# Memory scores at a place of their own, V's transposes in another PSUM bank, shifted start eighths for the first halves, and query loads of later chunks on SyncE's queue

## The chip, the cores and the metric

The kernel runs on one core of a Trainium2 chip. The metric is the device time of one execution in microseconds. In the text PE is TensorE's matmul stream, PEld its weight loads, DVE VectorE, ACT ScalarE, POOL GpSimd and SP SyncE.

## What is computed

One layer of a decoder, float32. Cut to what matters here (one sequence of 4096 tokens, d_model 1024; 64 sample tokens, the keys and values of the memory and the state of the convolution are treated beside it):

```python
h = rmsnorm(x, g_pre);  z = h @ w_in          # one projection, columns split in groups
out_a = silu(cg) * cb * conv3(cc * ch)        # 256 channels
out_b = silu(ag) * window_attention(q, k, v)  # 8 query heads, 2 kv heads, head_dim 64,
                                              # window 128, blocks of 128 queries, sink per head
out_c = silu(mg) * memory_attention(mq, mk, mv)  # 4 heads, 256 memory tokens
y = concat(out_a, out_b, out_c) @ w_out
return x + rmsnorm(y, g_post)
```

Window attention takes for each block of 128 queries the keys of this block and of the one before, masks them to a band, and adds a sink logit per head to the softmax. Memory attention is a plain softmax over 256 keys.

## The kernel before

**Stages.** The first 930 us or so are the input projection (lines 368 and 375): x is normalised and multiplied with `w_in` in three passes over groups of columns, in a seven-product scheme for blocks of 2 x 2, with every operand split into a high and a low float32r part. It writes to DRAM: `qd` (queries, keys, memory queries, as high and low parts), `vd` (V, transposed), `md` (the gates, and the finished convolution group). The attention of chunk 0 runs inside it. The last stage, from about 930 us to the end, is the output projection of all tokens with the attention of chunks 1 to 15 woven in.

**Chunks, halves, blocks, eighths.** A chunk c is 256 tokens. Half h = 2c + i is the attention of 128 of them (i is 0 or 1). A block is 128 rows of the output projection: `Block.run` multiplies a block with `w_out` in two parts of 512 columns (p = 0, 1), each with eight k steps of three matmuls of 512 columns (line 1602, tile y). A block has therefore 16 steps (p, k), called eighths here since each is an eighth of a part, and 48 matmuls. Before such a step the functions that are due are called: `starts_of(i)` looks them up by the running number 16 i + 8 p + k.

**What a half does.** `first_half(h)` and `second_half(h)` hold it. The first half of the work:

- `memory_transposes` of half h - 1 (tile xt, line 1352): the memory probabilities xp are transposed on TensorE into a PSUM bank pair of tag x, and copied out by VectorE and ScalarE (xpt, line 1356).
- `window_scores` of half h (ws, line 1318): 16 matmuls into two bank pairs of tag w.
- `products` of half h - 1 (wo, lines 1376, 1382 and 1057): probabilities times values, window and memory, into a bank pair of tag x.
- In a chunk's first half, two TensorE transposes that turn V's tile vT into tokens by channels (line 1654); they go into the unused end of the bank pair of the products, and ScalarE copies them out with a factor 0.5 (vt, line 1664).
- `window_probabilities` of half h: ScalarE copies the scores (sm, line 1327), VectorE merges the band (1328) and takes maxima (1266, 1268), ScalarE the exponentials (1274), VectorE the shares (1279 to 1282). In their midst the block before is finished (`finish_block(True)`, line 1624: row scaling and residual, in xr). `gates` (lines 1240, 1393) multiplies the products into the tile mix.
- the loads of the next chunk (`chunk_load`), or of the mix tile of the next chunk.

The second part:

- `memory_scores` (xs, line 1340): eight matmuls into a bank pair of tag x; maxima on VectorE (xmx, line 1155; negated in xnm, line 1156), exponentials on ScalarE (xp, line 1164), the reciprocal on VectorE (xrd, line 1170), the scaling on POOL (line 1176).
- `window_turns` (wt, line 1364): eight transposes of the window probabilities into a bank pair of tag w, ScalarE copies them (wpt, line 1292), and POOL masks them into two triangles (wpv and wpt, lines 1297 and 1300). The products of the next first half read both.

There are two bank pairs of tag w, one of tag x, and two single banks of tag z for y. So in the x pair xt, wo and xs follow one another in turn.

**Order.** TensorE runs in the order written (a manual schedule up to block 25); the other engines' orders, and SP's and POOL's queues, come from a list scheduler at build time. Each queue works in its order, and a DMA that waits holds up what is behind it. The split of the next block's mix tile into high and low parts (mh on ScalarE, line 1583; ml on VectorE, line 1584) is also started from `starts_of`.

**Loads.** Even chunks keep their keys (kst) and queries (q) in one buffer each, odd chunks in another, so that the loads of chunk c + 1 wait for the last reads of chunk c - 1. Keys and queries go by POOL's DMA queue (four DMAs, line 1086, and six of 256 KB, line 1099), vT, mix, xr and the output stores by SP's (lines 1089, 1108, 1569, 1627).

Of the kernel before, what the change touches and what calls it, by code (L numbers as in the profile page):

```python
# [15 lines left out]
P = 128  # L16
# [10 lines left out]
CT = 256  # L27
NCH = 4096 // CT
# [19 lines left out]
def f(ap):  # L48
    return ap.bitcast(F32)
# [3 lines left out]
def hybrid_layer(ctx: ExitStack, tc: tile.TileContext, a: dict):  # L53
    nc = tc.nc
    TE, V, S, G, DMA = nc.tensor, nc.vector, nc.scalar, nc.gpsimd, nc.sync
# [7 lines left out]
    ident = const.tile([P, P], F32, name="ident")  # L63
# [939 lines left out]
    chunks = {}  # L1003
# [37 lines left out]
    def two_banks(tag, name):  # L1041
        return ps[tag].tile([P, 2, 512], F32, tag=tag, name=name)
# [23 lines left out]
    class Chunk:  # L1066
# [24 lines left out]
        def load_queries(self):  # L1091

            self.q = self.pool("q").tile([P, 12, CT], F32R, tag="q", name=f"q{self.c}")
            heads = lambda part, j, ts: qd[part, j : j + 2, :, ts].rearrange("j (v d) n -> d j v n", v=2)
            for part in range(2):

                for n, (i, j) in enumerate(((0, 1), (4, 3), (8, 5))):
                    half = (n == 2) ^ part
                    G.dma_start(self.q[64 * half : 64 * half + 64, i : i + 4, :].rearrange("p (j v) n -> p j v n", v=2),  # L1099
                                heads(part, j, self.ts))  # L1100

        def load_mix(self):

# [291 lines left out]
    def chunk_load(c):  # L1395
        if c < NCH:
            chunks[c] = Chunk(c)

            chunks[c].load_queries() if c == 2 else chunks[c].load_keys()
            chunks[c].load_keys() if c == 2 else chunks[c].load_queries()  # L1400
# [238 lines left out]
    def first_half(h):  # L1639

        c, i = divmod(h, 2)
        before = (chunks[(h - 1) // 2], (h - 1) % 2) if 2 < h <= 2 * NCH else None
        if before:
            before[0].memory_transposes(before[1])
        if c < NCH:
            chunks[c].window_scores(i)
        banks = before[0].products(before[1]) if before else None
        new_v = c < NCH and i == 0
        if new_v:
            chunks[c].values(chunks[c - 1].vts[2])  # L1650
            banks = two_banks("x", f"vtp{c}") if banks is None else banks
            t = [banks[:, 1, CT + n * P : CT + n * P + P] for n in range(2)]
            for n in range(2):
                TE.transpose(t[n], chunks[c].vT[:, n * P : n * P + P], ident)
        soon = first_at[h] > 16 * (h - 3) + 4
        if before and soon:
            before[0].gates(before[1], banks)
        if c < NCH:
            chunks[c].window_probabilities(i)
        if before and not soon:  # L1660
            before[0].gates(before[1], banks)
        if new_v:
            for n in range(2):
                S.mul(chunks[c].vts[1 + n], t[n], 0.5)
            chunk_load(c + 1)
        elif c + 1 < NCH:
            chunks[c + 1].load_mix()

    def second_half(h):

        c, i = divmod(h, 2)
        if c < NCH:
            chunks[c].memory_scores(i)
            chunks[c].window_turns(i)


    first_at = {2: 4, 3: 21, 4: 35, 5: 47, 6: 59, 7: 71} | {h: 16 * (h - 3) + 4 for h in range(8, 2 * NCH + 1)}
    second_at = {2: 14, 3: 27, 4: 40, 5: 52, 6: 64, 7: 76} | {h: first_at[h] + 8 for h in range(8, 2 * NCH + 1)}

    def starts_of(i):  # L1680

        at = [(n, lambda h=h: first_half(h)) for h, n in first_at.items()] + [(n, lambda h=h: second_half(h)) for h, n in second_at.items()]
        if i + 1 < len(blocks) and blocks[i + 1].b != 32:
            at.append((max(16 * i, first_at.get(i + 2, 0) + 2), blocks[i + 1].split))
        return {(p, k): lambda now=now: [fn() for fn in now] for p in range(2) for k in range(8)
                if (now := [fn for n, fn in at if n == 16 * i + 8 * p + k])}
# [26 lines left out]
    for i in range(31):  # L1713
        if i == 26:
            turn.close()
        starts = starts_of(i)
        for step in ((p, k) for p in range(2) for k in (1, 3)) if i >= 26 else ():
            starts[step] = lambda before=starts.get(step, lambda: None): (before(), late())
        run(i, starts)
    for stage in stages:  # L1720
        for _ in stage:
            pass
    run(31, starts_of(31))
    run(32, {})
    finish_block()
# [106 lines left out]
```

## Time and profile before

| | us |
|---|---|
| Runs shown | 1541.38, 1549.06, 1551.43 (median 1549.06) |
| The profiled execution, whole | 1542.05 |
| Its span, first to last instruction | 1540.3 |
| TensorE matmuls busy | 1520.7 |
| TensorE weight loads busy (beside the matmuls) | 1397.0 |
| VectorE, ScalarE, POOL busy | 1137.5, 791.0, 393.2 |

How it is read: the profile comes from one execution, and its sums are sums of that execution. TensorE's busy time includes the modelled end of each matmul, which overlaps the next one, so the mean of a matmul is longer than the distance between two. The profile's waits are attributed to the instruction that released last. A weight load (PEld) precedes its matmul and runs beside the matmul before it, so that a wait for an operand of a transpose shows first in the weight loads. In a window's row stand, after the two ends, the length, then busy time (and instructions) of PE, PEld, DVE, ACT and POOL, the granted TensorE clock, the busy share of the DMA engines, and GB/s.

### The profile page before, as it was taken

Reading aid. Unit: us, or ns where it says so; the run is one execution under the profiler, and the core shown is the slowest. Engines: PE = TensorE matmul, PEld = TensorE weight load, DVE = VectorE, ACT = ScalarE, POOL = GpSimd, SP = SyncE. Lnnn points to the kernel's source line nnn. Section 1 sums busy time; section 2 is a strip of 40 time slices with the busy share of each in tenths; the row PEclk is TensorE's granted clock in tenths of the full one; section 3 lists DMA queues with packets and bytes.
Section 4 is the critical chain, followed back from the end, with each engine's and each line's share of the span. In section 5 each row is a group of like instructions: output and inputs, shape, how many; then the busy total and the mean of one; then the engine's idle time right before and its main releaser. Section 6 shows DMA issues by size and latency. Waiting matters only on the chain.

```text
span 1540.3 us, 30416 instructions
## 1 busy us (share of the span) xinstructions
PE 1520.7 (99%) x11581; PEld 1397.0 (91%) x11581; DVE 1137.5 (74%) x1965; ACT 791.0 (51%) x1949; POOL 393.2 (26%) x635
## 2 busy tenths in 40 slices
PE   9999999999999999999999999999999999999998
PEld 9999999999999999999999998778888888888776
DVE  6789887899988777897677678666666666666653
ACT  6686665476222222445454456555555555555541
POOL 0223232211400000000101203554444444445410
PEclk9999999999999999999999999999999999999999
DMA  9999999878755333678876889967777666666332
GB/s 258 177 240 232 278 284 263 276 241 292 193 180 180 126 126 126 236 223 281 244 269 204 238 295 272 208 140 155 156 155 161 149 149 160 148 148 150 124 123 96
DMA packets 178453, 306.29 MB, mean 199 GB/s; under 512 B 34437, under 2 KB 108165, under 8 KB 178277
## 3 DMA queue, kind: packets, MB, share of 16 engines
q1 hardware_dynamic: 130901, 227.38, 48.2%
q0 software_dynamic: 46688, 75.93, 23.5%
q8 instruction: 91, 1.49, 0.4%
q10 hardware_dynamic: 720, 1.05, 0.2%
q14 instruction: 53, 0.43, 0.1%
HBM read 197.23 MB, written 108.05 MB: 198 GB/s over the span
## 4 chain that ended last, share of the span: by engine, by line
PE 76%; DMA 7%; DVE 5%; POOL 5%; ACT 4%; issue 3%; ACTq 0%; SPq 0%; DVEq 0%; POOLq 0%
PE c L368 47%; PE y L1602 15%; DMA nat<-in_x_p 3%; PE ws L1318 3%; POOL xp L1176 3%; PE wo L1382 2%; PE wo L1057 2%; PE xs L1340 1%; PE wt L1364 1%; PE xt L1352 1%; DMA md<-th 1%; PE wo L1376 1%; POOL wpt L1300 1%; ACT xp L1164 1%; DMA x_0B<-in_xt 1%
## 5 line engine op out<-in xcount | busy, mean ns | idle before, releaser
L1602 PE MATMUL y<-wo,mh 128*128 128x512 f32 (+1 forms) x1040 | 336.1, 394 | 0.0
L375 DVE TENSOR_TENSOR z<-c,z 128x520 f32<-128x520 f32 (+1 forms) x308 | 194.8, 646 | 82.2 <-PE c L368 80.3
L1602 PEld LDWEIGHTS y<-wo,mh 128*128 128x128 f32 x1040 | 194.3, 188 | 42.3 <-issue 4.4
L1602 PE MATMUL y<-wo,ml 128*128 128x512 f32 (+1 forms) x520 | 201.4, 387 | 0.0
L1274 ACT ACTIVATE sm<-sm,wnm 128x128 f32<-128x128 f32 x256 | 99.4, 390 | 70.4 <-DVE wnm L1268 70.4
L1602 PEld LDWEIGHTS y<-wo,ml 128*128 128x128 f32 x520 | 98.0, 188 | 17.7
L1099 POOL DMA_DIRECT2D q<-qd x96 | 59.8, 631 | 139.2 <-PE wt L1364 81.6
L1176 POOL TENSOR_SCALAR xp<-xp,xrd 128x256 f32<-128x256 f32 x128 | 84.9, 675 | 34.8 <-DVE xrd L1170 34.7
L1297 POOL TENSOR_SCALAR_AFFINE_SELECT wpv<-wpt 128x512 f32<-128x512 f32 x62 | 40.4, 665 | 145.4 <-ACT wpt L1292 145.3
L1328 DVE COPY_PREDICATED sm<-wmask,ws 128x512 f32<-128x512 uint8 x60 | 40.6, 732 | 38.2 <-ACT sm L1327 38.2
L737 POOL CAST wmask<-negs 128x256 uint8<-128x256 f32 x1 | 0.9, 930 | 265.8 <-DMA negs<-in_wmask 265.8
L1292 ACT COPY wpt<-wt 128x512 f32<-128x512 f32 x64 | 34.6, 589 | 64.2 <-PE wt L1364 64.2
L1164 ACT ACTIVATE xp<-xs,xnm 128x256 f32<-128x256 f32 x128 | 59.4, 488 | 9.0 <-DVE xnm L1156 6.7
L1155 DVE TENSOR_REDUCE xmx<-xs 128x2 f32<-128x512 f32 x64 | 41.5, 686 | 29.9 <-PE xs L1340 29.8
L1356 ACT COPY xpt<-xt 128x512 f32<-128x512 f32 x30 | 17.6, 586 | 87.3 <-DVE xpt L1356 87.3
L1609 DVE TENSOR_TENSOR yn<-y,gpost 128x512 f32<-128x512 f32 (+1 forms) x66 | 45.1, 683 | 22.1 <-PE y L1602 22.0
L1318 PE MATMUL ws<-kst,q 128*128 128x256 f32 (+1 forms) x480 | 55.8, 298 | 0.0
L276 ACT ACTIVATE nat<-nat 104x1024 f32<-104x1024 f32 x40 | 42.3, 1058 | 26.1 <-DMA nat<-in_x_p 26.1
L1610 ACT ACTIVATE y<-y 128x512 f32<-128x512 f32 (+1 forms) x66 | 39.3, 595 | 30.2 <-DVE yn L1609 30.2
L1300 POOL TENSOR_SCALAR_AFFINE_SELECT wpt<-wpt 128x512 f32<-128x512 f32 x64 | 42.1, 669 | 43.3 <-ACT wpt L1292 43.1
L1356 DVE COPY xpt<-xt 128x512 f32<-128x512 f32 x30 | 20.8, 692 | 42.5 <-PE xt L1352 42.4
L1086 POOL DMA_DIRECT2D kst<-qd x64 | 38.8, 625 | 51.5 <-issue 24.8
(976 smaller groups left out, 5135.5 us busy)
## 6 DMA issues: line engine op xcount, KB each, us to landing
q<-qd POOLq DMA_DIRECT2D x96, 256.0 KB, 4.7
xr<-in_x_p SPq DMA_DIRECT2D x32, 512.0 KB
nat<-in_x_p SPq DMA_DIRECT2D x39, 416.0 KB
o_yp<-xr SPq DMA_DIRECT2D x31, 512.0 KB
md<-th POOLq DMA_DIRECT2D x48, 260.0 KB, 6.6
qd<-zh SPq DMA_DIRECT2D x48, 260.0 KB
qd<-z SPq DMA_DIRECT2D x48, 260.0 KB
kst<-qd POOLq DMA_DIRECT2D x60, 192.0 KB, 4.6
```

What stands on the lines that cost most here:

```text
L276: S.activation(t[:RG], t[:RG], AF.Square, accum_out=r[:RG, i : i + 1])
L368: TE.matmul(bank[:, :HW], l, r, start=first and i == 0, stop=last and i == 3 * KH - 1)
L375: add = lambda dst, other: V.tensor_tensor(dst, c, other, op=ALU.add)
L1099: G.dma_start(self.q[64 * half : 64 * half + 64, i : i + 4, :].rearrange("p (j v) n -> p j v n", v=2), heads(part, j, self.ts))
L1155: V.tensor_reduce(mx[:, :nb], s, axis=AX.X, op=ALU.max)
L1164: S.activation(p[:, i, :], s[:, i, :], AF.Exp, bias=nm[:, i : i + 1], scale=SCALE, accum_out=den[:, i : i + 1])
L1176: G.tensor_scalar(p[:, i, :], p[:, i, :], self.rds[h][:, i : i + 1], 0.5, op0=ALU.mult, op1=ALU.mult)
L1274: S.activation(sm[:, hh, :], sm[:, hh, :], AF.Exp, bias=nm[:, hh : hh + 1], scale=SCALE, accum_out=den[:, hh : hh + 1])
L1300: G.affine_select(p3, p3, pattern=[[0, 4], [1, P]], compare_op=ALU.is_ge, fill=0.0, base=0, channel_multiplier=-1)
L1318: TE.matmul(out(kvh, col, bank), q(kvh, col, bank)[r], k(kvh, part)[r], start=first, stop=True, skip_group_check=not first, **place)
L1602: TE.matmul(acc, self.hl[l][:, k], wo[k][c0 // 512][:, r, c0 % 512 : c0 % 512 + c1 - c0], start=j == 0, stop=j == passes * KT - 1)
L1609: V.tensor_tensor(yn[:m, c0:c1], acc[:m], gpost[:m, c0:c1], op=ALU.mult)
```

## The change

Four edits, all in the last stage:

1. `memory_scores` leaves `second_half` and becomes `memory_half(h)`, which is called at a time of its own: six eighths after the first half from h = 8 on (the second half stays at eight), five (seven for h = 2) before that.
2. V's transposes leave `first_half` and stand in `second_half` behind `window_turns`, in a bank pair of tag w instead of the end of a pair of tag x. Their copies on ScalarE stand right behind them.
3. The start eighths of halves 3 to 5, and the second starts of halves 4 to 7, are shifted. From half 8 on first and second starts are the same.
4. The six query loads of chunks 2 to 15 are issued on SP's queue; those of chunks 0 and 1 stay with POOL.

```diff
@@ load_queries
                     half = (n == 2) ^ part
-                    G.dma_start(self.q[64 * half : 64 * half + 64, i : i + 4, :].rearrange("p (j v) n -> p j v n", v=2),
-                                heads(part, j, self.ts))
+                    dst, src = self.q[64 * half : 64 * half + 64, i : i + 4, :].rearrange("p (j v) n -> p j v n", v=2), heads(part, j, self.ts)
+                    if self.c > 1:
+                        DMA.dma_start(f(dst), f(src))
+                    else:
+                        G.dma_start(dst, src)
@@ first_half
         banks = before[0].products(before[1]) if before else None
-        new_v = c < NCH and i == 0
-        if new_v:
-            chunks[c].values(chunks[c - 1].vts[2])
-            banks = two_banks("x", f"vtp{c}") if banks is None else banks
-            t = [banks[:, 1, CT + n * P : CT + n * P + P] for n in range(2)]
-            for n in range(2):
-                TE.transpose(t[n], chunks[c].vT[:, n * P : n * P + P], ident)
...
-        if new_v:
-            for n in range(2):
-                S.mul(chunks[c].vts[1 + n], t[n], 0.5)
+        if c < NCH and i == 0:
             chunk_load(c + 1)
...
-    def second_half(h):
+    def memory_half(h):
 
         c, i = divmod(h, 2)
         if c < NCH:
             chunks[c].memory_scores(i)
+
+    def second_half(h):
+
+        c, i = divmod(h, 2)
+        if c < NCH:
+            if i == 0:
+                chunks[c].values(chunks[c - 1].vts[2])
             chunks[c].window_turns(i)
+            if i == 0:
+                t = two_banks("w", f"vtp{c}")[:, 0].rearrange("p (a n) -> p a n", a=4)
+                for n in range(2):
+                    TE.transpose(t[:, n], chunks[c].vT[:, n * P : n * P + P], ident)
+                for n in range(2):
+                    S.mul(chunks[c].vts[1 + n], t[:, n], 0.5)
...
-    first_at = {2: 4, 3: 21, 4: 35, 5: 47, 6: 59, 7: 71} | {h: 16 * (h - 3) + 4 for h in range(8, 2 * NCH + 1)}
-    second_at = {2: 14, 3: 27, 4: 40, 5: 52, 6: 64, 7: 76} | {h: first_at[h] + 8 for h in range(8, 2 * NCH + 1)}
+    first_at = {2: 4, 3: 19, 4: 33, 5: 46, 6: 59, 7: 71} | {h: 16 * (h - 3) + 4 for h in range(8, 2 * NCH + 1)}
+    memory_at = {2: 11, 3: 24, 4: 38, 5: 51, 6: 64, 7: 76} | {h: first_at[h] + 6 for h in range(8, 2 * NCH + 1)}
+    second_at = {2: 14, 3: 27, 4: 41, 5: 54, 6: 67, 7: 79} | {h: first_at[h] + 8 for h in range(8, 2 * NCH + 1)}
...
+        at += [(n, lambda h=h: memory_half(h)) for h, n in memory_at.items()]
```

On TensorE the order of a half from 8 on was: xt, ws, wo, (V's transposes), 24 y matmuls, xs, wt, 24 y. It becomes: xt, ws, wo, 18 y, xs, 6 y, wt, (V's transposes), 24 y. In ScalarE's built order the copies of wt now stand behind the exponentials of the memory scores, and in POOL's order the scaling of xp stands ahead of the four masks.

More of the change, by code (lines that the diff above doesn't have):

```diff
@@ L1667, in first_half @@
             chunks[c + 1].load_mix()
+    def memory_half(h):
+        c, i = divmod(h, 2)
+        if c < NCH:
+            chunks[c].memory_scores(i)
     def second_half(h):
@@ L1672, in second_half @@
         if c < NCH:
-            chunks[c].memory_scores(i)
+            if i == 0:
+                chunks[c].values(chunks[c - 1].vts[2])
             chunks[c].window_turns(i)
-    first_at = {2: 4, 3: 21, 4: 35, 5: 47, 6: 59, 7: 71} | {h: 16 * (h - 3) + 4 for h in range(8, 2 * NCH + 1)}
-    second_at = {2: 14, 3: 27, 4: 40, 5: 52, 6: 64, 7: 76} | {h: first_at[h] + 8 for h in range(8, 2 * NCH + 1)}
+            if i == 0:
[7 more added lines that the diff above has]
+    second_at = {2: 14, 3: 27, 4: 41, 5: 54, 6: 67, 7: 79} | {h: first_at[h] + 8 for h in range(8, 2 * NCH + 1)}
     def starts_of(i):
         at = [(n, lambda h=h: first_half(h)) for h, n in first_at.items()] + [(n, lambda h=h: second_half(h)) for h, n in second_at.items()]
+        at += [(n, lambda h=h: memory_half(h)) for h, n in memory_at.items()]
         if i + 1 < len(blocks) and blocks[i + 1].b != 32:
```

## The prediction

> **What bounds the kernel now.** I read the page first, then busy time by stage, then who held up TensorE's weight loads, then the timelines of the last stage. A "half" below is the attention work of 128 tokens. Its TensorE sections carry the tile names xt (transposes of the memory probabilities), ws (window scores), wo (products), xs (memory scores) and wt (transposes of the window probabilities); y, the output projection, runs between them.
>
> ```profile
> span 1540.3 us, 30416 instructions
> PE 1520.7 (99%) x11581; PEld 1397.0 (91%) x11581; DVE 1137.5 (74%) x1965; ACT 791.0 (51%) x1949; POOL 393.2 (26%) x635
> ...
> 929.00:1035.00 106.00, 101.28 (x666) 81.58 (x665) 75.27 (x173) 63.11 (x222) 50.34 (x86) 1.00 0.94 222
> 1035.00:1426.00 391.00, 388.31 (x2558) 315.45 (x2557) 256.35 (x593) 217.47 (x778) 188.63 (x299) 1.00 0.69 152
> 1426.00:1540.00 114.00, 107.31 (x704) 84.76 (x702) 62.14 (x147) 46.69 (x155) 24.33 (x50) 0.99 0.34 115
> ```
>
> TensorE sets the time: 99% busy, at full granted clock (third column from the right). The change touches only the stage from about 930 us on, and there TensorE idles 4.7, 2.7 and 6.7 us. Most of the last is the tail behind the last matmul, which the change leaves alone. But busy time includes the modelled drain of a matmul, so a wait shorter than a drain is not seen as idle. The weight loads show it (who waited for whom: us in total, times, longest). The first four lines are from 930 to 1035 us, the last from 1035 to 1426:
>
> ```profile
> PEld xt L1352 <- POOL xp L1176: 5.0, 8, 1.2
> PEld xs L1340 <- ACT vt L1664: 1.9, 2, 0.9
> PEld wt L1364 <- issue: 1.2, 3, 0.5
> PEld wt L1364 <- ACT y L1610: 0.3, 1, 0.3
> ...
> PEld xt L1352 <- POOL xp L1176: 10.3, 35, 0.6
> ```
>
> So xt waits for POOL's scaling of the memory probabilities all along, xs waited twice for ScalarE's copy of V's transposes, and wt waited a little at the start. On the matmuls themselves (start, duration):
>
> ```profile
> 1109.55 1.65 PE L1352 MATMUL xt<-ident,xp 128*128 128x128 f32 x8
> 1110.95 1.86 PE L1318 MATMUL ws<-kst,q 128*128 128x256 f32 x16
> ...
> 1128.26 1.29 PE L1352 MATMUL xt<-ident,xp 128*128 128x128 f32 x8
> 1129.31 1.86 PE L1318 MATMUL ws<-kst,q 128*128 128x256 f32 x16
> ...
> 1462.57 1.06 PE L1352 MATMUL xt<-ident,xp 128*128 128x128 f32 x8
> 1463.39 1.86 PE L1318 MATMUL ws<-kst,q 128*128 128x256 f32 x16
> ```
>
> From the start of xt to the start of ws are 1.40 us in a chunk's first half, 1.05 in its second, and 0.82 where nothing is waited for. So 0.58 and 0.23 us are lost in turn.
>
> **Term 1: the wait at xt, steady halves.** Why is xp late? POOL's timeline, with VectorE's split of the next block (ml) between:
>
> ```profile
> 1103.65 0.62 POOL L1099 DMA_DIRECT2D q<-qd  x1 [6.68 <-PE wt L1364]
> 1105.55 0.61 POOL L1099 DMA_DIRECT2D q<-qd  x1
> 1106.61 0.93 POOL L1176 TENSOR_SCALAR xp<-xp,xrd 128x256 f32<-128x256 f32 x2 [0.45 <-DVE xrd L1170]
> 1108.19 1.61 DVE L1584 TENSOR_TENSOR ml<-mix,mh 128x1024 fp32r<-128x1024 f32 x1 [0.40 <-ACT mh L1583]
> 1108.71 1.89 POOL L1176 TENSOR_SCALAR xp<-xp,xrd 128x256 f32<-128x256 f32 x2
> ...
> 1123.71 1.23 POOL L1297 TENSOR_SCALAR_AFFINE_SELECT wpv<-wpt 128x512 f32<-128x512 f32 x2 [9.53 <-ACT wpt L1292]
> 1126.10 2.85 POOL L1176 TENSOR_SCALAR xp<-xp,xrd 128x256 f32<-128x256 f32 x4
> ```
>
> In one kind of half two query loads (1.23 us of POOL) stand ahead of xp, in the other all four window masks do. The change takes both away: queries go to SyncE, xs moves two eighths of a block (six y matmuls) ahead of wt, and in the built order POOL then scales xp before the masks. I follow one half from the start of ws:
>
> ```profile
> 1117.97 0.42 DVE L1393 TENSOR_TENSOR mix<-mix,wo 128x256 f32<-128x256 f32 x1
> 1120.12 0.69 DVE L1282 TENSOR_TENSOR sm<-sm,wrd 128x512 f32<-128x512 f32 x1
> 1120.98 1.11 PE L1340 MATMUL xs<-mk,q 128*128 128x256 f32 x8
> 1122.12 1.29 DVE L1155 TENSOR_REDUCE xmx<-xs 128x2 f32<-128x512 f32 x2 [1.31 <-PE xs L1340]
> 1125.07 0.17 DVE L1170 RECIPROCAL xrd<-xden 128x2 f32<-128x2 f32 x1 [1.46 <-ACT xp L1164]
> ```
>
> With ws at 0 (1110.95), xs now starts at 10.0; six y matmuls and V's transposes earlier it starts at about 8.5. The x bank it writes is freed by the gate's end at 7.4, so 1.1 us are to spare. VectorE is held until 9.9 by the softmax and then takes the maxima. The first reciprocal comes 2.95 later, at 12.8, so xp runs from about 13.1 to 15.9, even with one slow pair (0.93 + 1.89). The next xt starts at 17.4: 1.5 us to spare, the wait goes. The group row bounds the gain above by 10.3; below, 22 halves at 0.58 and 0.23 in turn give 8.9. I take **-9.6**.
>
> Masks come later than before: wt's copies now follow the exponentials on ScalarE, POOL's masks run from 15.9 to about 18.5 (four of 0.62), and wo needs them at 18.2 + 3.3 = 21.5. So that cover holds by 3 us; without it each us late is a us on TensorE.
>
> A page of the Trainium skill speaks against the margin: SBUF — State Buffer, section "Who interferes with whom", has a VectorE operation with two SBUF inputs (ml is one) and a POOL operation that reads SBUF block each other for the whole instruction. The trace agrees: two xp take 0.93 alone, 1.89 beside ml. If both pairs met such work, xp would end at 16.9 and still beat xt, by 0.5 us; the sum stays.
>
> **Term 2: the early halves (2 to 7).** They follow one another after 12 to 14 eighths of a block instead of 16. The four early rows add to 8.4 us; TensorE's idle time there, 4.7, is the floor; I take 7 as what is lost now. The wait on ACT goes with the move of V's transposes to a w bank (their copy then gates only a bank that is next written a half later). wt gets 8 eighths after ws instead of 5. What remains is VectorE's order, here of half 5:
>
> ```profile
> 993.95 1.22 DVE L1584 TENSOR_TENSOR ml<-mix,mh 128x1024 fp32r<-128x1024 f32 x1
> 996.27 1.64 DVE L1624 SCALAR_TENSOR_TENSOR xr<-yn,yst,xr 128x1024 f32<-128x1024 f32 x1 [0.43 <-POOL yst L1616]
> 997.84 0.60 DVE L1156 TENSOR_SCALAR xnm<-xmx 128x2 f32<-128x2 f32 x1
> ```
>
> The second negated maximum stands behind ml and the block's finish (2.9 us), and in the built order still does in half 5; in half 6 only behind ml. I leave 0.7 us each at two of the xt: **-5.5**, with -1 (memory chain still late everywhere) and -8.4 as bounds.
>
> **Term 3: more switches.** Every y run that is interrupted pays once:
>
> ```profile
> 1133.58 0.50 PE L1602 MATMUL y<-wo,mh 128*128 128x512 f32 x1
> 1139.15 1.11 PE L1340 MATMUL xs<-mk,q 128*128 128x256 f32 x8
> ...
> 1454.17 0.50 PE L1602 MATMUL y<-wo,mh 128*128 128x512 f32 x1
> 1454.99 1.11 PE L1340 MATMUL xs<-mk,q 128*128 128x256 f32 x8
> ```
>
> 24 y matmuls took 5.57 us, 3 took 0.82: 0.226 each plus 0.14 for the run. All 30 halves from 2 on get one run more, and the built order shows three more in the sample work after 1448: 33 x 0.14 = **+4.6**. Bounds: 0, if the pause only fills what another wait would have taken, and 5.6 at 0.17.
>
> **Edits at nothing.** V's two transposes and copies keep their cost (same instructions, other place); they are covered by the half that passes before wo uses them. The six query loads per chunk keep their bytes; SyncE pays the issues.
>
> ```profile
> 948.20 0.81 SPq L1569 DMA_DIRECT2D xr<-in_x_p  x2
> 950.15 4.22 SPq L1089 DMA_DIRECT2D vT<-vd  x1
> ...
> 1062.41 0.34 SPq L1627 DMA_DIRECT2D o_yp<-xr  x1
> 1065.05 0.33 SPq L1569 DMA_DIRECT2D xr<-in_x_p  x1
> ...
> q<-qd POOLq DMA_DIRECT2D x96, 256.0 KB, 4.7
> ```
>
> On SyncE the first query load waits until xs has read the old queries, with the next xr load, then the output store behind it. It is released about when that xr load is issued now, and xr is needed a block (18 us) or more later; a delay of 1 to 2 us is covered. The new queries are needed over two halves later, against 4.7 us to land. Tight only once: chunk 2's, five of them issued behind the xr loads at 949. With a blocked issue like the 4.22 and twice 4.7 they land by about 963; half 4 needs them at about 966. Cost 0, bound +3 once. Five queries less ahead of xr make xr earlier, if anything.
>
> **Sum:** -9.6 - 5.5 + 4.6 = -10.5 on the profiled execution's own 1542.05 us (span 1540.3 and 1.75 around it): 1531.5. Its time is at the low end of the runs shown (1541.38, 1549.06, 1551.43); scaled to their median, 1549.06 x 1531.5 / 1542.05 = **1538.5**.
>
> **Rivals**, on the median's scale. (a) Fuller gain: the pause at a switch is absorbed and no early wait stays: -10.3 - 8.4 = -18.7, 1530. For it: xs would no longer press on the bank; against: 0.14 stands behind every run in the trace. Over 1% faster. (b) The waits stay: xp is late again because VectorE's finish or split cuts into xmx as in half 5. Then only the two ACT waits go (-1.9) and the switches cost 4.6: +2.7, 1552. For it: 2.9 us of such work is more than the 1.5 spare; against: in the built order of the steady halves xmx and xnm stand ahead of both. (c) Slower: xs meets the x bank before the gates have freed it. It decides from 1.1 us later gates on, and every half then pays; in-order TensorE holds the y behind it. At 2 us later, 24 halves pay 0.9 each, 21.6, so +11 in all: 1560. From 1.55 us on the kernel is slower than before. For it: the gate stands behind the 1.28 us finish on VectorE, which waits for POOL's power of the row sum, now behind the masks; against: the power ends at about 19.1, so 0.9 into the next half, and the finish needs it only 5 into it. (d) The forecast with queries of chunk 2 late by 3: 1541.5, in the range.
>
> **Chances:** forecast with (d) 0.70, (a) 0.14, (b) 0.10, (c) 0.06. Own range of the forecast, by the bounds: -18.7 to -4.3, so 1530 to 1545; the runs shown spread by 10 us, so 80% needs 1527 to 1553, which takes in (a) and (b). About 1% (15.5 us) is what a measurement of this kernel can tell. Faster by over that: (a) and a share of the forecast by the runs' spread, 0.20; slower: (c) and a little of (b), 0.07; between 0.73.
>
> **What would show it.** Right: weight loads of xt no longer wait for xp in steady halves and xt to ws is near 0.82; no wait of xs on vt; a pair of halves takes 36.4 us instead of 36.9; y runs of 18 and 6 before and after xs; POOL with no query loads after chunk 1. Wrong: xs waiting for VectorE's gates, wo for masks, or ws of half 4 for a query load.

## The result and the profile after

The changed kernel takes 1530.61 us (median of six runs, 1528.48 to 1536.75), the kernel before 1547.24 beside it (median of six, 1541.38 to 1551.43): a ratio of 0.9899, 95% interval 0.987 to 0.9929. So it is faster by about 1%, which lies at the edge of what a measurement of this kernel can tell. The forecast was 1538.5, range 1527 to 1553. The profiled execution took 1528.56 us (1542.05 before), and all the readings below go by its trace.

The page's head and the busy time by stage, with the columns of the rows of before (ends, length, busy time of PE, PEld, DVE, ACT and POOL with their instructions, granted clock, DMA share, GB/s):

```profile
span 1526.8 us, 30582 instructions
PE 1513.8 (99%) x11581; PEld 1397.6 (92%) x11581; DVE 1136.3 (74%) x1965; ACT 793.0 (52%) x1949; POOL 339.6 (22%) x551
...
929.00:1035.00 106.00, 103.46 (x699) 84.57 (x697) 74.25 (x176) 63.77 (x225) 40.06 (x69) 1.00 0.92 231
1035.00:1415.00 380.00, 379.88 (x2546) 313.03 (x2542) 256.42 (x591) 219.86 (x779) 145.96 (x232) 1.00 0.62 154
1415.00:1527.00 112.00, 105.87 (x685) 83.56 (x681) 61.88 (x146) 45.72 (x153) 21.76 (x50) 0.99 0.34 116
```

TensorE has the same 11581 matmuls, and its idle time in the middle stage is down to 0.1 us (2.7 before). Who held up the weight loads (us in total, times, longest), first from 929 to 1035 us:

```profile
PEld xt L1355 <- POOL xp L1179: 3.0, 5, 1.5
...
PEld wt L1367 <- issue: 0.6, 1, 0.6
PEld wt L1367 <- ACT y L1613: 0.5, 1, 0.5
```

then from 1035 to 1420 us, the whole answer:

```profile
PEld wo L1385 <- issue: 8.5, 22, 0.4
PEld y L1605 <- issue: 3.8, 22, 0.2
PEld wo L1379 <- issue: 0.3, 1, 0.3
```

The wait of xt for xp (10.3 us before) is gone from the steady halves. In the early halves the two waits of xs for ScalarE's copy of V (1.9 us before) are gone too, and 3.0 us at xt are left.

One half of the changed kernel on TensorE (start, duration; part of the y matmuls left out):

```profile
1087.09 1.86 PE L1321 MATMUL ws<-kst,q 128*128 128x256 f32 x16
...
1095.58 1.11 PE L1343 MATMUL xs<-mk,q 128*128 128x256 f32 x8
1096.53 0.39 PE L1605 MATMUL y<-wo,mh 128*128 128x512 f32 x1
1096.76 0.40 PE L1605 MATMUL y<-wo,ml 128*128 128x512 f32 x1
...
1097.91 1.03 PE L1367 MATMUL wt<-ident,sm 128*128 128x128 f32 x8
1098.70 0.47 PE L1605 MATMUL y<-wo,mh 128*128 128x512 f32 x1
1099.02 0.40 PE L1605 MATMUL y<-wo,ml 128*128 128x512 f32 x1
...
1104.28 1.03 PE L1355 MATMUL xt<-ident,xp 128*128 128x128 f32 x8
1105.07 1.86 PE L1321 MATMUL ws<-kst,q 128*128 128x256 f32 x16
1106.86 0.43 PE L1379 MATMUL wo<-wpv,vt 64*64 64x256 f32 x2
```

From xt to ws are 0.79 us (1104.28 to 1105.07), below even the 0.82 that the forecast took for a half without a wait.

For the accounts below I cut TensorE's timeline into sections, each from its start to the start of the next, and added them by kind over two stretches: the *early stretch*, from the first y matmul to ws of half 8, and the *steady stretch*, from there to ws of half 30 (22 halves).

| us | early | steady | of steady: xt | y (runs) | wt + V | xs |
|---|---|---|---|---|---|---|
| before | 106.12 | 406.63 | 27.30 | 244.94 (44) | 19.55 | 20.84 |
| after | 101.77 | 398.13 | 17.38 | 245.84 (66) | 19.79 | 20.80 |

The span is 13.5 us shorter: 4.35 in the early stretch, 8.50 in the steady one, 0.5 behind ws of half 30, 0.1 ahead of the first y. The 0.5 are the difference of two: TensorE takes 0.6 us longer in the sample work there, and the end behind its last matmul is 1.1 us shorter (7.0 to 5.9). The first stage holds no edit, yet it ends at different times. The first y matmul in the trace above and in a second one of the same kernel:

```profile
930.82 0.39 PE L1605 MATMUL y<-wo,mh 128*128 128x512 f32 x1
```

```profile
927.91 0.39 PE L1605 MATMUL y<-wo,mh 128*128 128x512 f32 x1
```

Those are 2.9 us apart, of the 3.1 by which the two spans differ. Over all traces of this text, whose kernels are edited in the last stage alone, the first y starts between 927.9 and 935.7 us. So the experiments are judged by the two stretches.

### The profile page after: what moved, and what is told of

It is laid out like the page before. It is cut to its first block, busy times and chain, and to the rows that moved or that the text cites. A ratio compares the mean times of both kernels' runs of the same rounds, so it can differ in the third digit from the quotient of the medians.

```text
span 1526.8 us, 30582 instructions
## 1 busy us (share of the span) xinstructions
PE 1513.8 (99%) x11581; PEld 1397.6 (92%) x11581; DVE 1136.3 (74%) x1965; ACT 793.0 (52%) x1949; POOL 339.6 (22%) x551
## 3 DMA queue, kind: packets, MB, share of 16 engines
q10 hardware_dynamic: 720, 1.05, 0.2%
## 4 chain that ended last, share of the span: by engine, by line
PE 84%; DMA 6%; DVE 4%; ACT 3%; issue 1%; POOL 1%; ACTq 0%; SPq 0%; DVEq 0%; POOLq 0%
PE c L368 46%; PE y L1605 23%; PE ws L1321 3%; DMA nat<-in_x_p 3%; PE wo L1385 2%; PE wo L1057 2%; PE xs L1343 2%; PE xt L1355 2%; PE wt L1367 2%; DMA md<-th 1%; PE wo L1379 1%; PE mem_acc L789 1%; DMA x_0B<-in_xt 1%; DMA wr_2A<-in_w_in 1%; ACT sm L1277 0%
## 5 line engine op out<-in xcount | busy, mean ns | idle before, releaser
L1605 PE MATMUL y<-wo,mh 128*128 128x512 f32 (+1 forms) x1040 | 341.6, 394 | 0.0
L1179 POOL TENSOR_SCALAR xp<-xp,xrd 128x256 f32<-128x256 f32 x128 | 61.6, 494 | 273.0 <-DVE xrd L1173 272.5
L1303 POOL TENSOR_SCALAR_AFFINE_SELECT wpt<-wpt 128x512 f32<-128x512 f32 x64 | 62.4, 994 | 43.7 <-ACT wpt L1295 43.1
L407 ACT CAST zh<-z 128x520 fp32r<-128x520 f32 x56 | 33.3, 624 | 35.5 <-DVE z L375 31.9
L377 ACT COPY z<-c 128x520 f32<-128x520 f32 (+1 forms) x44 | 24.4, 554 | 51.5 <-PE c L368 47.8
L1321 PEld LDWEIGHTS ws<-kst,q 128*128 128x128 f32 (+1 forms) x480 | 46.5, 187 | 4.1
L1277 ACT ACTIVATION_READ_ACCUMULATOR sm<-sm,wnm 128x1 f32 x256 | 47.8, 187 | 0.0
L1173 DVE RECIPROCAL xrd<-xden 128x2 f32<-128x2 f32 x64 | 10.6, 166 | 49.2 <-ACT xp L1167 49.2
```

Of the source, the lines that this page charges most:

```text
L1179: G.tensor_scalar(p[:, i, :], p[:, i, :], self.rds[h][:, i : i + 1], 0.5, op0=ALU.mult, op1=ALU.mult)
L1277: S.activation(sm[:, hh, :], sm[:, hh, :], AF.Exp, bias=nm[:, hh : hh + 1], scale=SCALE, accum_out=den[:, hh : hh + 1])
L1303: G.affine_select(p3, p3, pattern=[[0, 4], [1, P]], compare_op=ALU.is_ge, fill=0.0, base=0, channel_multiplier=-1)
L1321: TE.matmul(out(kvh, col, bank), q(kvh, col, bank)[r], k(kvh, part)[r], start=first, stop=True, skip_group_check=not first, **place)
L1605: TE.matmul(acc, self.hl[l][:, k], wo[k][c0 // 512][:, r, c0 % 512 : c0 % 512 + c1 - c0], start=j == 0, stop=j == passes * KT - 1)
```

## The experiments

**The theory and its rivals.** xt waited for POOL's scaling. The theory: the scores' own turn takes that wait away, since xs comes earlier and POOL scales ahead of the masks. Rivals: the query loads on POOL were the cause; V's move is needed too; and, on the price, that every interrupted run of y pays 0.14 us.

| us | early | steady | of steady: xt | y (runs) | wt + V | xs | median, ratio to before (95%) |
|---|---|---|---|---|---|---|---|
| the changed kernel again | 101.69 | 397.97 | 17.38 | 245.89 (66) | 19.76 | 20.80 | 1527.80, 0.9891 (0.9871 to 0.9912) |
| queue only | 104.46 | 402.49 | 23.06 | 244.91 (44) | 19.53 | 20.87 | 1538.41, 0.9959 (0.9944 to 0.9974) |
| queue undone | 102.04 | 397.94 | 17.38 | 245.88 (66) | 19.80 | 20.78 | 1532.07, 0.9919 (0.9904 to 0.9934) |
| scores' turn undone | 107.10 | 400.45 | 20.56 | 245.29 (44) | 19.81 | 20.82 | 1537.42, 0.9949 (0.9932 to 0.9967) |
| V's move undone | 101.44 | 398.45 | 17.39 | 245.78 (66) | 19.51 | 21.75 | 1529.51, 0.9902 (0.9887 to 0.9917) |
| turn and eighths only | 101.35 | 398.43 | 17.38 | 245.69 (66) | 19.54 | 21.82 | 1532.44, 0.9928 (0.9904 to 0.9951) |
| old eighths | 105.95 | 397.98 | 17.42 | 245.87 (66) | 19.78 | 20.76 | 1533.48, 0.9936 (0.9918 to 0.9953) |
| scores in two pieces | 105.27 | 398.56 | 17.38 | 245.60 (88) | 19.80 | 20.64 | 1534.71, 0.9943 (0.9916 to 0.997) |
| transposes in two pieces | 100.18 | 398.15 | 17.39 | 247.85 (88) | 17.97 | 20.78 | 1527.55, 0.9907 (0.9878 to 0.9935) |
| other eighths | 99.89 | 399.93 | 17.37 | 245.90 (66) | 19.80 | 20.77 | 1530.15, 0.9896 (0.9877 to 0.9916) |
| other eighths, transposes in two | 99.83 | 398.42 | 17.37 | 247.83 (88) | 17.98 | 20.80 | 1530.71, 0.9903 (0.9881 to 0.9924) |

The first row is the changed kernel unaltered, and "queue only" is the kernel before with one edit. The others are the changed kernel with one thing altered, but for "turn and eighths only", which undoes two edits, and the last row, which joins two alterations.

**The changed kernel again.**

> The changed kernel itself once more, beside the two next ones. 0.988 to 0.992 of the kernel before; early stretch 101.8, steady stretch 398.1.

As expected: both stretches repeat within 0.2 us, while the spans differ by 3.1 (1523.7 and 1526.8).

**Queue only.**

```diff
@@ kernel before, load_queries
-                    G.dma_start(self.q[64 * half : 64 * half + 64, i : i + 4, :].rearrange("p (j v) n -> p j v n", v=2),
-                                heads(part, j, self.ts))
+                    dst, src = ...  # the same two, by name
+                    if self.c > 1:
+                        DMA.dma_start(f(dst), f(src))
+                    else:
+                        G.dma_start(dst, src)
```

> The kernel before, with only the query loads of chunk 2 and later moved to SyncE's queue. My theory: the wait at xt is set by where POOL's scaling of the memory probabilities stands behind other work, and by when xs starts. With the loads gone, the built order puts all four window masks ahead of the scaling in every half, as the kernel before has it in a chunk's second half only; so each xt of the steady halves waits about 0.23 us, where the first halves waited 0.58 and the second 0.23. That is 11 x 0.35 = 3.9 us less over the 22 steady halves (ws of half 8 to ws of half 30: 406.6 to about 402.7), the early halves about as before (106.1, at most 1 less), the two waits of xs for ScalarE's copy of V stay. In all about 4 us under the kernel before. Rival (the loads on POOL were the whole cause): no xt waits in the steady halves any more, 398 to 397 there, about 9 to 10 us under the kernel before. Rival (only the place of xs counts): no change, 406 to 407.

Measured: 402.49 in the steady stretch, 0.2 from the number of my theory; the rivals gave 397 to 398 and 406 to 407. The weight loads from 1040 to 1430 us:

```profile
PEld xt L1355 <- POOL xp L1179: 6.0, 23, 0.3
```

Each half now waits as a chunk's second half did. So the queue carries 4.1 us of the 8.5 when it is alone, and xt goes on waiting. The early stretch is 1.7 us shorter than before, more than the 1 that was expected at most.

**Queue undone.**

```diff
@@ changed kernel, load_queries
-                    dst, src = ...
-                    if self.c > 1:
-                        DMA.dma_start(f(dst), f(src))
-                    else:
-                        G.dma_start(dst, src)
+                    G.dma_start(self.q[64 * half : 64 * half + 64, i : i + 4, :].rearrange("p (j v) n -> p j v n", v=2),
+                                heads(part, j, self.ts))
```

> The changed kernel, with all query loads on POOL's queue again. My theory: the place of xs takes away the wait alone. In the built order the scaling stands ahead of the masks and at most two query loads, 0.65 us each, come ahead of it; its measured margin at xt in the steady halves is over 1.3 us. So 398.1 us for the 22 steady halves again, at most 1 more, no xt wait there, and the whole within 1 us of the changed kernel (1528.6). Rival (the loads were the cause): the wait at xt is back in each first half, 11 x 0.4 to 0.6, so 402.5 to 404.7 in the steady stretch and 4 to 6 us over the changed kernel.

Measured: 397.94, no xt wait, as my theory had it. The loads stand ahead of the scaling again, but fit into the time in which POOL would wait for the reciprocal:

```profile
1097.79 1.24 POOL L1099 DMA_DIRECT2D q<-qd  x2 [5.29 <-PE xs L1340]
1100.46 1.85 POOL L1176 TENSOR_SCALAR xp<-xp,xrd 128x256 f32<-128x256 f32 x4 [1.43 <-DVE xrd L1170]
```

The profiled execution (1530.61 us) is 2.1 us above the changed kernel's, where 1 was expected at most; 1.1 of that lie behind the last matmul (see "Edits at nothing" below).

**Scores' turn undone.**

```diff
@@ changed kernel
-        at += [(n, lambda h=h: memory_half(h)) for h, n in memory_at.items()]
@@ second_half
+            memory_half(h)
             if i == 0:
                 chunks[c].values(chunks[c - 1].vts[2])
```

> The changed kernel, with the memory scores issued right ahead of the transposes of the window probabilities again (no run of their own, the eighths of the transposes as changed, V's transposes and the queue as changed). My theory: xs 1.4 us later and the masks ahead of the scaling again, so xt waits about 0.23 in each steady half: 22 x 0.23 = 5.1 us more, less 22 x 0.04 for the y run that is saved: 398.1 to about 402.3 in the steady stretch. The early halves with 2 to 3 us more of xt waits. In all 5 to 7 us over the changed kernel, still 6 to 8 under the kernel before. Rival (each interrupted y run costs 0.14, as I forecast): 22 x 0.14 = 3.1 saved in the steady stretch, so 400.1 there, and 33 x 0.14 = 4.6 in all, so only 2 to 3 over the changed kernel. Rival (the loads were the whole cause): no xt wait in the steady stretch, 397 or less.

Measured: 400.45, close to the number of the rival with 0.14, but for another reason: the y sections fell by 0.55 us for 22 runs less, 0.025 each, where that rival needs 3.1. What is smaller than my theory had it is the wait: xt gained 3.2 instead of 5.1, since only every other half waits. POOL's rows show the masks ahead of a scaling that takes 2.85 us instead of 1.85 (its pairs meet ml again), and below them stand the weight loads from 1040 to 1430 us:

```profile
1108.26 1.23 POOL L1303 TENSOR_SCALAR_AFFINE_SELECT wpt<-wpt 128x512 f32<-128x512 f32 x2
1109.48 2.85 POOL L1179 TENSOR_SCALAR xp<-xp,xrd 128x256 f32<-128x256 f32 x4
```

```profile
PEld xt L1355 <- POOL xp L1179: 3.1, 12, 0.3
```

The early stretch came out 5.3 us longer than in the changed kernel, and longer than in the kernel before: expected were 2 to 3. So the new eighths without the scores' turn are a loss.

**V's move undone.**

```diff
@@ changed kernel, first_half
+        new_v = c < NCH and i == 0
+        if new_v:
+            chunks[c].values(chunks[c - 1].vts[2])
+            banks = two_banks("x", f"vtp{c}") if banks is None else banks
+            t = [banks[:, 1, CT + n * P : CT + n * P + P] for n in range(2)]
...
+            for n in range(2):
+                S.mul(chunks[c].vts[1 + n], t[n], 0.5)
@@ second_half (V's transposes and copies taken out)
```

> The changed kernel, with V's transposes in the first half and in the x bank again, as before. My theory: ScalarE's copy of V then stands between the gate and xs in each chunk: the copy ended 8.6 us after the start of ws in the kernel before, and xs now wants to start at 8.5 to 8.7. So xs waits 0.1 to 0.4 in each chunk's first half: 11 x 0.25 = about 2.7 us more in the steady stretch (398.1 to about 400.9), and 0.5 to 1 us in each of three early halves; rows of xs waiting for ACT vt come back. In all 2 to 6 us over the changed kernel. Rival (the copy is early enough everywhere, the move was for nothing): within 1 us of the changed kernel, no xs wait on vt.

My theory fell. The wait that it named is there, in each chunk (from 1035 to 1430 us):

```profile
PEld xs L1343 <- ACT vt L1667: 3.2, 11, 0.7
```

but the 3.2 us of weight-load waits lengthen the xs sections by 0.95 only, and V's transposes cost 0.28 less in their old place: 398.45, and the early stretch 0.3 shorter. The time is the rival's, though it expected no such wait.

**Turn and eighths only.**

```diff
@@ V's move undone, and the queue undone: in load_queries
-                    dst, src = ...
-                    if self.c > 1:
-                        DMA.dma_start(f(dst), f(src))
-                    else:
-                        G.dma_start(dst, src)
+                    G.dma_start(...)
```

> The changed kernel, with V's transposes in the first half and the x bank and the queries on POOL, both as before: what is left of the change is the memory scores' own turn and the new eighths. Each of the two edits alone undone gave 397.9 and 398.5 us in the steady stretch (398.1 in the changed kernel) and 102.0 and 101.4 in the early one (101.8). My theory: the place of the scores alone carries the gain: 398 to 399 steady, 101 to 102.5 early, within 1.5 us of the changed kernel. Rival (each of the two edits covers for the other): with both undone the query loads and V's copy stand ahead of the scaling together, xt waits again in each chunk's first half, 11 x 0.3 to 0.6, 401.4 to 404.7 in the steady stretch and 3 to 7 us over the changed kernel.

Measured: 398.43 and 101.35, as my theory had it. The scores' turn with its eighths carries 8.2 of the 8.5 us in the steady stretch and all of the early gain; the queue and V's move add nothing that shows in these two stretches. There they matter only where the turn is missing: queue alone leaves 402.5, queue and V's move 400.5.

**Old eighths.**

```diff
-    first_at = {2: 4, 3: 19, 4: 33, 5: 46, 6: 59, 7: 71} | {...}
-    memory_at = {2: 11, 3: 24, 4: 38, 5: 51, 6: 64, 7: 76} | {...}
-    second_at = {2: 14, 3: 27, 4: 41, 5: 54, 6: 67, 7: 79} | {...}
+    first_at = {2: 4, 3: 21, 4: 35, 5: 47, 6: 59, 7: 71} | {...}
+    memory_at = {2: 12, 3: 25, 4: 38, 5: 50, 6: 62, 7: 74} | {...}
+    second_at = {2: 14, 3: 27, 4: 40, 5: 52, 6: 64, 7: 76} | {...}
```

> The changed kernel, with the eighths of the early halves (2 to 7) as before: first parts at 21, 35, 47, 59, 71, transposes at 14, 27, 40, 52, 64, 76, memory scores two eighths ahead of them. My theory: the steady stretch stays (398.1). In the early stretch (101.8 in the changed kernel) the memory scores have 8 to 9 eighths until the next half's xt instead of 7 to 9, but the transposes only 5 behind ws again; the softmax is then late for the transposes at two or three halves, 0.3 to 0.5 each, and VectorE's order puts the second maximum behind the block's finish: early 102.5 to 104.5, 1 to 3 us over the changed kernel in all. Rival (the eighths do nothing, the scores' own turn does all): within 0.5 of 101.8.

The direction was right and the size too small: 4.2 us longer. The weight loads from 930 to 1037 us, and VectorE and TensorE at one of the waits:

```profile
PEld wt L1367 <- issue: 5.6, 4, 2.3
```

```profile
994.70 0.68 DVE L1158 TENSOR_REDUCE xmx<-xs 128x2 f32<-128x512 f32 x1
...
995.38 0.69 DVE L1158 TENSOR_REDUCE xmx<-xs 128x2 f32<-128x512 f32 x1
...
996.19 0.69 DVE L1285 TENSOR_TENSOR sm<-sm,wrd 128x512 f32<-128x512 f32 x1
```

```profile
997.03 0.63 PE L1367 MATMUL wt<-ident,sm 128*128 128x128 f32 x4 [0.66 <-DVE sm L1285]
```

With xs ahead of wt, VectorE takes both maxima before the last share of the softmax, and wt waits for that share. At the longest of these waits (2.1 us, half 4) ml stands ahead of the share as well. In the early stretch neither the turn with the old eighths (105.95) nor the new eighths without the turn (107.10) does as well as the queue's move alone (104.46); together they give 101.77, and 101.35 without the queue's and V's moves.

**Scores in two pieces.**

```diff
@@ changed kernel
-        at += [(n, lambda h=h: memory_half(h)) for h, n in memory_at.items()]
+        at += [(n + piece, lambda h=h, piece=piece: memory_half(h, piece)) for h, n in memory_at.items() for piece in range(2)]
@@ memory_scores
-            for h in range(4):
+            for h in range(2 * piece, 2 * piece + 2):
...
+            if piece == 0:
+                return
```

> The changed kernel, with the memory scores cut into two pieces of four matmuls, one eighth (three y matmuls) apart: one more interrupted y run in each half, and the maxima, exponentials and scaling start one eighth (0.7 us) later. In the traces of the kernel before and of the changed kernel, y, the window transposes and V's transposes of the 22 steady halves take 264.5 and 265.6 us with 44 and 66 y runs, so one run more costs 0.05. My theory: the switch costs what these say, 22 x 0.05 = 1.1 us more in the steady stretch (398.1 to about 399.2), and no xt wait, since the scaling has over 1.3 us to spare. In all 1 to 2 us over the changed kernel. Rival (0.14 for each interrupted run, as I forecast): 22 x 0.14 = 3.1 in the steady stretch, 401.2, and over 4 in all. Rival (the later scaling meets xt): xt waits come back, 0.2 or more in each half, 4 us or more, and the weight loads show them.

**Transposes in two pieces.**

```diff
@@ changed kernel
-        at = ... + [(n, lambda h=h: second_half(h)) for h, n in second_at.items()]
+        at = ... + [(n + piece, lambda h=h, piece=piece: second_half(h, piece)) for h, n in second_at.items() for piece in range(2)]
@@ window_turns
-            for kvh in range(2):
-                for hh in range(4):
-                    TE.transpose(tw[:, kvh, hh * P : (hh + 1) * P], self.sms[kvh][:, hh, :], ident)
+            for hh in range(4):
+                TE.transpose(tw[:, piece, hh * P : (hh + 1) * P], self.sms[piece][:, hh, :], ident)
+            if piece == 0:
+                return
```

> The changed kernel, with the transposes of the window probabilities cut into two pieces of four, one eighth apart: one more interrupted y run in each half, this one behind transposes. A y run behind transposes shows 0.32 us from its first to its second matmul where one behind the memory scores shows 0.23. My theory: what stands ahead of y decides, so this run costs 0.10 to 0.13: 22 x 0.10 to 22 x 0.13, 2.2 to 2.9 us more in the steady stretch (398.1 to 400.3 to 401.0), more than the run behind the memory scores (1.1). Rival (each run costs the same, 0.05): 399.2. Rival (0.14 for each, as I forecast): 401.2. Masks come one eighth later and still ahead of the products, so nothing else moves.

Both settle the price of an interrupted run, below what any of the theories had. TensorE's timelines, scores in two and then transposes in two:

```profile
1102.05 0.39 PE L1609 MATMUL y<-wo,mh 128*128 128x512 f32 x1
...
1102.75 0.63 PE L1345 MATMUL xs<-mk,q 128*128 128x256 f32 x4
```

```profile
1096.17 0.60 PE L1368 MATMUL wt<-ident,sm 128*128 128x128 f32 x4
1096.52 0.48 PE L1608 MATMUL y<-wo,mh 128*128 128x512 f32 x1
...
1097.30 0.60 PE L1368 MATMUL wt<-ident,sm 128*128 128x128 f32 x4
```

Three y matmuls behind the scores take 0.70 us (1102.05 to 1102.75), where 3 x 0.226 is 0.68. Behind transposes they take 0.78 (1096.52 to 1097.30): a pause of 0.10. But four transposes take 0.35 and eight took 0.79 in the changed kernel (1097.91 to 1098.70), so cutting them gives back 0.09. In the steady stretch y grew by 2.0 and wt with V fell by 1.8: 398.15 against 398.13. With the scores in two, the steady stretch has 0.43 more, of which 0.86 is a single wait at half 8, and no xt wait; y and xs are 0.4 less. So a further interruption costs nothing here that can be seen. In the early halves, though, the later second piece of the scores cost 3.5 us (the scaling comes too late for halves 6 and 7), and the transposes in two gained 1.6, at xt and wt.

**Other eighths, and both.**

```diff
@@ changed kernel
-    first_at = {2: 4, 3: 19, 4: 33, 5: 46, 6: 59, 7: 71} | {...}
-    memory_at = {2: 11, 3: 24, 4: 38, 5: 51, 6: 64, 7: 76} | {...}
-    second_at = {2: 14, 3: 27, 4: 41, 5: 54, 6: 67, 7: 79} | {...}
+    first_at = {2: 4, 3: 19, 4: 33, 5: 46, 6: 59, 7: 72} | {...}
+    memory_at = {2: 12, 3: 24, 4: 38, 5: 50, 6: 63, 7: 76} | {...}
+    second_at = {2: 15, 3: 27, 4: 41, 5: 54, 6: 67, 7: 80} | {...}
```

> The changed kernel with a few early eighths moved: half 7's first part at 72 instead of 71, memory scores of halves 2, 5 and 6 at 12, 50 and 63 instead of 11, 51 and 64, transposes of halves 2 and 7 at 15 and 80 instead of 14 and 79. Left in the early stretch of the changed kernel are 0.7 us at the transposes of half 2, and 1.05 and 1.84 at the xt of halves 6 and 7. My theory: these are lost only because the memory chain starts too late for its half; one eighth of 0.7 us more on each takes away 0.7 at half 2, all of half 6's and at least 1.2 of half 7's, so the early stretch takes 99 to 100 instead of 101.8, the steady one 398.1, and the whole is 2 us under the changed kernel. Rival (the wait follows VectorE's order, not the start): scores one eighth earlier meet the block's finish or the softmax, and the wait moves to the transposes: 101.5 or more.

> The moved early eighths and the transposes cut in two, together, the latter having given an early stretch of 100.2 and a steady one of 398.2. My theory: the remaining waits, 1.0 and 0.5 us at the xt of halves 6 and 7, go: early 98.5 to 99.5, steady 398.2, about 3 us under the changed kernel. Rival (cut and eighths take away the same waits and the cut costs its switches): no better than the eighths alone.

The early stretch did what my theory said (99.89), and the steady one gave it back (399.93 instead of 398.1), at one place: wo of half 8, on TensorE, POOL and VectorE:

```profile
1033.84 1.86 PE L1321 MATMUL ws<-kst,q 128*128 128x256 f32 x16
1037.68 0.43 PE L1379 MATMUL wo<-wpv,vt 64*64 64x256 f32 x2 [1.98 <-ACT xpt L1359]
```

```profile
1032.84 1.21 POOL L1300 TENSOR_SCALAR_AFFINE_SELECT wpv<-wpt 128x512 f32<-128x512 f32 x2
1034.02 1.22 POOL L1303 TENSOR_SCALAR_AFFINE_SELECT wpt<-wpt 128x512 f32<-128x512 f32 x2
```

```profile
1033.60 2.72 DVE L1587 TENSOR_TENSOR ml<-place,mh 128x1024 fp32r<-128x1024 f32 x1 [1.69 <-ACT mh L1586]
1036.24 0.68 DVE L1359 COPY xpt<-xt 128x512 f32<-128x512 f32 x1
```

One eighth later, half 7's masks, which have started first, meet ml, which takes 2.72 us instead of 1.23; the copy of xt stands behind ml on VectorE, ScalarE's part of that copy behind VectorE's, and the products wait for it. Neither theory had that. The version with both missed its own 98.5 to 99.5 in the early stretch: at 99.83 it is no better than the eighths alone, as the rival had it. But at half 8 it has no such stall (0.3 us of weight-load waits for the masks), and its two stretches together are 1.7 us shorter than the changed kernel's (498.25 against 499.90), as are those of the transposes in two alone (498.33). Medians of 1530.71, 1527.55 and 1527.80 do not tell them from the changed kernel, so none of these is shown to beat it.

## Why the prediction was right or wrong

**Term 1 (forecast -9.6): right, -9.9.** The xt sections of the 22 steady halves fell from 27.30 to 17.38. The steps held: with ws at 0 (1087.09) xs started at 8.49 (forecast 8.5), and the gates ended at 7.3 (forecast 7.4):

```profile
1094.02 0.41 DVE L1396 TENSOR_TENSOR mix<-mix,wo 128x256 f32<-128x256 f32 x1
...
1102.61 1.67 DVE L1587 TENSOR_TENSOR ml<-mix,mh 128x1024 fp32r<-128x1024 f32 x1 [0.16 <-ACT mh L1586]
```

```profile
1099.57 1.85 POOL L1179 TENSOR_SCALAR xp<-xp,xrd 128x256 f32<-128x256 f32 x4 [7.88 <-DVE xrd L1173]
1101.38 1.22 POOL L1300 TENSOR_SCALAR_AFFINE_SELECT wpv<-wpt 128x512 f32<-128x512 f32 x2
1102.56 2.21 POOL L1303 TENSOR_SCALAR_AFFINE_SELECT wpt<-wpt 128x512 f32<-128x512 f32 x2
```

The margin at xt was better than forecast: xp ran from 12.5 to 14.3 (forecast 13.1 to 15.9) with xt at 17.2, so 2.9 us to spare instead of 1.5. None of the 88 scalings in the steady stretch overlaps ml any more, where 33 did before; the last masks do (2.21 instead of 1.22). The Trainium skill's rule on VectorE's and POOL's shared port (SBUF — State Buffer, section "Who interferes with whom": whichever has the port holds the other up for its whole instruction) agrees with these rows and with the 2.72 above; the collision was moved, not removed. Over the whole kernel one xp went from 675 to 494 ns, one of the second masks from 669 to 994:

```profile
L1176 POOL TENSOR_SCALAR xp<-xp,xrd 128x256 f32<-128x256 f32 x128 | 84.9, 675 | 34.8 <-DVE xrd L1170 34.7
L1300 POOL TENSOR_SCALAR_AFFINE_SELECT wpt<-wpt 128x512 f32<-128x512 f32 x64 | 42.1, 669 | 43.3 <-ACT wpt L1292 43.1
```

```profile
L1179 POOL TENSOR_SCALAR xp<-xp,xrd 128x256 f32<-128x256 f32 x128 | 61.6, 494 | 273.0 <-DVE xrd L1173 272.5
L1303 POOL TENSOR_SCALAR_AFFINE_SELECT wpt<-wpt 128x512 f32<-128x512 f32 x64 | 62.4, 994 | 43.7 <-ACT wpt L1295 43.1
```

One number of the margin was wrong: the products start 1.8 us behind ws (1106.86 against 1105.07), not 3.3, which is where the last of them start. The masks end at 17.7 and are needed at 19.8: a cover of 2.1 us, not 3. It still held. And the reason was too wide: the forecast named the query loads beside the place of xs, and the runs showed that the place is enough. Its own rows say as much: the two loads ended at 1106.16, and the first pair of xp still waited until 1106.61 for the reciprocal. What held the second pair, in the kernel before, are two masks ahead of it, and then ml:

```profile
1107.50 0.63 POOL L1300 TENSOR_SCALAR_AFFINE_SELECT wpt<-wpt 128x512 f32<-128x512 f32 x1
1108.09 0.63 POOL L1297 TENSOR_SCALAR_AFFINE_SELECT wpv<-wpt 128x512 f32<-128x512 f32 x1
```

**Term 2 (-5.5, with six switches -4.7): right in size, -4.35, by luck.** The two parts that make it up were both too small, and their errors cancel. After: 0.9 us at and just ahead of wt of half 2 and 1.05 and 1.84 at xt of halves 6 and 7 remain, 3.8 where 1.4 was left. Before: 4.35 + 3.8 is about 8 us lost, near the upper bound of 8.4 and not the 7 taken. What held it was found by the runs: the turn needs the eighths and the eighths the turn.

**Term 3 (+4.6): the step that failed.** In the steady stretch y, wt and V's transposes grew from 264.49 to 265.63, 1.1 us for 22 runs more, at most 0.05 each where 0.14 was taken (about 0.3 of the 1.1 belong to V's new place, by the run with V's move undone). The 0.14 came from two runs of y, one of 24 and one of 3 matmuls, and was put down as the price of any interruption. Behind the scores there is next to no pause (0.23 us from the first y matmul to the second, 1096.53 to 1096.76, against 0.32 behind the transposes, 1098.70 to 1099.02), and where there is one, cutting gave as much back in the transposes. In the steady stretch this is 3.1 - 1.1 = 2.0 us, most of the 3.0 by which the sum missed the trace (-10.5 against -13.5). Its lower bound, 0, was nearer.

**Edits at nothing: right on the cost, wrong on the queue's gain.** V's move costs nothing and brings nothing. Chunk 2's queries were not late: no wait of ws at half 4 shows. But the forecast took the tail behind the last matmul to be left alone, and there the queue's move brings 1.1 us. The profile shows three instructions called DRAIN at the end of POOL's stream, of which the first is the longest. The rows give their shortest, median and longest time in ns and their first and last start (kernel before, queue undone, changed kernel):

```profile
L1809 POOLq DRAIN  x3: 40/93/5340, 1534.2 to 1540.0; - x3
L1815 POOLq DRAIN  x3: 40/93/5342, 1522.4 to 1528.3; - x3
L1818 POOLq DRAIN  x3: 40/102/2972, 1521.8 to 1526.5; - x3
```

At 5.34 us it ends 0.85 us behind the last work of SyncE ahead of the common close (1539.53 and 1538.68), and the end waits for it; at 2.97 it ends ahead of SyncE's (1524.78 and 1526.06). In all traces, the three kernels with the query loads on POOL have 5.34 and 7.0 us from the last matmul to the end, the ten without have 2.97 and 5.9. Why the DRAIN is shorter is open.

**The rivals.** (a), the full gain of -18.7, half came about: the pause is all but absorbed, yet early waits stay. In the trace, -13.5 lies nearer to the forecast's -10.5; on the median, 1530.6 is (a)'s 1530, at the edge of the forecast's own range of 1530 to 1545, and the gain of 16.6 us is over the 15.5 to which the forecast gave 0.20. (b) and (c) did not; xs never waited for the gates. The scale to the median added 7 us to the forecast because the profiled execution of before lay at the low end of three runs. The shift by trace was -13.5 and by medians -16.6; the first stage's spread covers the difference. So of the 7.9 us between 1538.5 and 1530.6, 3.0 belong to the sum.

## What to carry to other kernels

When an in-order engine waits for a chain on others, first move the chain's start: here one earlier section of eight matmuls did alone, in the steady halves, what a queue and a bank did only in part. Price an interruption by the whole of the work on both sides of it, since a pause behind one section can be time missing from that section. A tighter schedule has several margins at once, and starting one part 0.7 us later cost 2 us of wait at the next half. And when work leaves a queue, look at the end of the kernel too.

## What was not expected of the hardware

A weight-load wait is no price: xs waited 3.2 us in 11 places and its sections grew by 0.95, while xt's 10.3 us of waits were worth 9.9. Why these differ is open. Four transposes of 128 x 128 took 0.35 us and eight 0.79, the y run behind either with the same pause of 0.10. And ml (1.23 us alone) took 2.72 beside masks of 0.6 that kept their own length, more than twice as long. POOL's closing DRAIN took 5.34 us with the query loads on its queue and 2.97 without, though the last of these loads lies far ahead of it (1408.25 against 1534.2 in the kernel before).
